# The reciprocal root of the first RMSNorm moves from the activations to the eviction of every projection bank

## The chip, the cores and the metric

The kernel runs on one core of a Trainium2 chip. The metric is the device time of one execution in microseconds (us); the runs are compared by their median. Engines are named as in the profile: PE is TensorE (matmuls; PEld its weight loads), DVE is VectorE, ACT is ScalarE, POOL is GpSimd, SP is the queue that issues most transfers.

## The reference

One layer of a hybrid decoder on 256 tokens of width 2048, all in fp32:

```python
n = rmsnorm(x, attn_norm[l])                 # x * rsqrt(mean(x*x) + eps) * attn_norm
u = n @ w_in[l]                              # 2048 -> 6928 columns
u_gdn, u_mlstm, u_rglru, u_rwkv = jnp.split(u, MIXER_SPLITS, axis=-1)
...                                          # four mixers, each a causal recurrence over the tokens
x = x + mix @ w_out[l]
n = rmsnorm(x, ffn_norm[l])
x = x + (jax.nn.silu(n @ ffn_w_gate[l]) * (n @ ffn_w_up[l])) @ ffn_w_down[l]
return rmsnorm(x, final_norm)
```

The reciprocal root is one number per token, so it can be multiplied in before the projection, on the activations, or after it, on each token's outputs. What the mixers do first with `u` matters here: gated delta rule (q, k, v) and mLSTM (q, k) put it through a causal convolution of four taps, RG-LRU puts one half through such a convolution with a bias and the other through a gelu, RWKV-7 mixes each token with the one before, and sixteen gate columns get a bias and go through softplus and the like.

## The kernel before, in words

**Products.** Every matrix product is made in three matmuls (`mm3`, lines 169 to 171) on operands split into a high and a low part: high x high, high x low, low x high. A weight block of 128 x 1024 is loaded by SP into one of four `raw` buffers, ACT copies its high part (`whi`) and DVE subtracts that to get the low part (`wlo`), lines 163 and 164. Both are issued through the helper `ch`, so the profile has them, and all else that `ch` issues, under lines 274 and 277. The activations lie transposed, 128 channels by 256 tokens in each of 16 tiles, as `nhi` and `nlo`.

**Input projection.** It goes in groups of 256 columns. A group takes four weight blocks and fills one PSUM bank of 512 columns (two halves of 128 channels by 256 tokens, or, with `tm=True`, two halves of 128 tokens by 256 channels). Three banks called `big` take turns. When a group is done its bank is emptied by a function decorated with `evict` (`shift_mix`, `conv`, `gelu2`, `silu2`), whose instructions are put 40 places forward in the priorities by which the order of work is laid out. That order is fixed when the program is built: a planner goes through the instructions by priority and by the times that it assumes, and gives each engine one list. Each engine then works through its list in order, and waits where an operand is not there.

**Start.** The sum of squares isn't known at first. So `setup` makes activations without the root (`un`: x times `attn_norm`, split into high and low, in four scratch pairs `UH`), and the first two groups (columns of the RWKV low-rank inputs and of r) run on them chunk by chunk as the transfers land. Meanwhile `squares` loads x once more in four pieces and sums the squares, `rstd` makes the root (`rs0`, one number per token on partitions), and `scales` spreads it by two matmuls over all partitions as the row `R` (128 x 256). The next two groups, k0 and v0, run on `un` too. The four banks are multiplied by `R` when `shift_mix` empties them (line 463). During v0, `normalise` (lines 282 to 290) makes the activations with the root: two multiplies on DVE (line 288), a copy to `nhi` on ACT (289) and a subtraction to `nlo` on DVE (290) for each pair of tiles. All later groups run on these, and their banks hold the finished `u`.

**Mixers.** Between weight blocks `group` calls `tick`, which steps generators: RWKV halves (`rw0`, `rw1`), RG-LRU, gates, delta rule and mLSTM halves, and two triangular solves on DVE (`solve_blocks`, lines 499 and 500). Their matmuls (line 409) take their places between the projection's in PE's list. After that come the output projection, the feed-forward part and the last norm; the change doesn't touch them.

**Lines of the evictions.** `shift_mix`: multiply 463 (first four banks), ACT copy 468, DVE 469. `conv`: ACT copy 759 or 761, three taps on DVE 763 for each half. `silu2`: 773, 774. `gelu2`: ACT 1165, 1166, then DVE 1167. Gates: 808. mLSTM v and output gate: 1430, 1433.

Of the kernel before, what the change touches and what calls it, by code (L numbers as in the profile page):

```python
# [7 lines left out]
F32 = mybir.dt.float32  # L8
F32R = mybir.dt.float32r
# [3 lines left out]
P = 128  # L13
T = 256
# [67 lines left out]
class Emitter:  # L82
# [115 lines left out]
    def setup(self):  # L198
        nc, A = self.nc, self.A
        self.pc = self.const([P, NCHAN], "chan")  # L200
        nc.scalar.dma_start(self.pc, A["chan"])
        c = 0
        for k, n in CHAN:
            self.PT[k] = self.pc[:, c : c + n]
            c += n
        ch = self.ch
        wu = self.const([P, 512], "wu", mybir.dt.bfloat16)
        ch("dve", nc.vector.memset, wu, 0.0)
        ch("act", nc.scalar.activation, self.const([P, 1], "wa"), wu[:, 0:1], AF.Square)
        z = self.mxl()  # L210
        for _ in range(WARM):
            ch("pe", nc.tensor.matmul, z, wu[:, 0:P], wu, start=True, stop=True)
        key = lambda g, c: ("w_in", 4 * c, 4, (RW + 1536, RW)[g], 256)
        raws, self.xt = {}, []

        def load(c):
            raws[0, c] = self.raw(*key(0, c))
            t = self.S(2)
            ch("sp", nc.sync.dma_start, t.rearrange("p (k t) -> p k t", k=4), A["xT"][:, 4 * c : 4 * c + 4, :])
            self.xt.append(t)  # L220
            raws[1, c] = self.raw(*key(1, c))

        load(0)
        load(1)
        self.nhi = self.xp.tile([P, KT, T], F32R, name="nhi", tag="nhi")
        self.nlo = self.xp.tile([P, KT, T], F32R, name="nlo", tag="nlo")
        self.UH = [(self.S(2), self.S(2)) for _ in range(4)]
        self.un = [tuple(t.bitcast(F32R)[:, (k % 4) * T : (k % 4) * T + T] for t in self.UH[k // 4]) for k in range(KT)]
        banks = [self.big(), self.big()]
        for c in range(4):  # L230
            ws = [self.halves(raws[0, c], *key(0, c))]
            for k in range(4 * c, 4 * c + 4):
                u, w = self.xt[c][:, (k % 4) * T : (k % 4) * T + T], self.PT["attn_norm"][:, k : k + 1]
                ch("act", nc.scalar.activation, self.un[k][0], u, AF.Copy, scale=w)
                ch("dve", nc.vector.scalar_tensor_tensor, self.un[k][1], u, w, self.un[k][0].bitcast(F32), op0=ALU.mult, op1=ALU.subtract)
            ws.append(self.halves(raws[1, c], *key(1, c)))
            for g, w in enumerate(ws):
                for l, r in ((0, 0), (0, 1), (1, 0)):
                    for m in range(2):
                        o = banks[g][:, m * T : m * T + T]  # L240
                        for kk in range(4):
                            k = 4 * c + kk
                            ch("pe", nc.tensor.matmul, o, w[l][:, kk, m * P : m * P + P], self.un[k][r], start=k == 0 and l == r == m == 0, stop=k == KT - 1 and l == 1, skip_group_check=True)
            if c < 2:
                load(c + 2)
        self.begun = self.chain
        self.chain = None
        self.ss = self.const([P, 2, 4], "ss")
        return banks

    def squares(self, c):

        nc = self.nc
        xs = self.S(2)
        nc.sync.dma_start(xs.rearrange("p (a n) -> p a n", a=2), self.A["x"].rearrange("(a p) d -> p a d", p=P)[:, :, c * 512 : c * 512 + 512])
        nc.scalar.activation(xs[:, 0:512], xs[:, 0:512], AF.Square, accum_out=self.ss[:, 0, c : c + 1])
        nc.vector.scalar_tensor_tensor(xs[:, 512:1024], xs[:, 512:1024], 1.0, xs[:, 512:1024], op0=ALU.mult, op1=ALU.mult, accum_out=self.ss[:, 1, c : c + 1])
        self.free(xs)
        if c == 3:
            self.rs0 = self.rstd(self.ss, "rs0")  # L260

    def scales(self, rs):

# [7 lines left out]
    def ch(self, key, fn, *a, **k):  # L271
# [6 lines left out]
        if self.chain is not None:  # L278
            self.chain[key] = i
        return i  # L280

    def normalise(self, u):

        nc = self.nc
        hi, lo = self.nhi[:, 2 * u : 2 * u + 2, :], self.nlo[:, 2 * u : 2 * u + 2, :]
        f = self.xt[u // 2].rearrange("p (k t) -> p k t", k=4)[:, 2 * (u % 2) : 2 * (u % 2) + 2, :]
        for j in range(2):
            nc.vector.scalar_tensor_tensor(f[:, j, :], f[:, j, :], self.PT["attn_norm"][:, 2 * u + j : 2 * u + j + 1], self.R[:, 0:T], op0=ALU.mult, op1=ALU.mult)
        nc.scalar.activation(hi, f, AF.Copy)
        nc.vector.tensor_tensor(lo, f, hi.bitcast(F32), op=ALU.subtract)  # L290

    def setup_consts(self):
        nc = self.nc
# [160 lines left out]
    return g  # L454


@evict
def shift_mix(em, bank, tiles, R=None):
    nc = em.nc
    X = em.S()  # L460
    if R is not None:
        b = em.S()
        nc.vector.tensor_tensor(b.rearrange("p (j t) -> p j t", j=2), bank.rearrange("p (j t) -> p j t", j=2), R[:, 0:T].unsqueeze(1).to_broadcast([P, 2, T]), op=ALU.mult)
        bank = b
    mu, mu1 = em.PT["rwkv_mu"], em.PT["mu1"]
    for j, ti in enumerate(tiles):
        u, o = bank[:, j * T : j * T + T], X[:, j * T : j * T + T]
        nc.scalar.activation(o, u, AF.Copy, scale=mu1[:, ti : ti + 1])
        nc.vector.scalar_tensor_tensor(o[:, 1:T], u[:, 0 : T - 1], mu[:, ti : ti + 1], o[:, 1:T], op0=ALU.mult, op1=ALU.add)
    if R is not None:  # L470
        em.free(b)
    return X


def rwkv_lora(em, bank):
    nc = em.nc
    X = shift_mix(em, bank, (12, 13), em.R)
    nc.scalar.activation(X[0:64, 0:T], X[0:64, 0:T], AF.Tanh)
    nc.scalar.activation(X[:, T : 2 * T], X[:, T : 2 * T], AF.Tanh, scale=0.5)
    nc.vector.tensor_scalar(X[:, T : 2 * T], X[:, T : 2 * T], 0.5, 0.5, op0=ALU.mult, op1=ALU.add)  # L480
    return X
# [270 lines left out]
def conv(em, bank, w, nt, tiles, bias=None):  # L752
    nc = em.nc
    X = em.S()
    for j, ti in enumerate(tiles):
        u, o = bank[:, j * T : j * T + T], X[:, j * T : j * T + T]
        tap = [w[:, i * nt + ti : i * nt + ti + 1] for i in range(4)]
# [3 lines left out]
            nc.scalar.activation(o, u, AF.Identity, scale=tap[3], bias=bias[:, ti : ti + 1])  # L761
        for d in range(1, 4):
            nc.vector.scalar_tensor_tensor(o[:, d:T], u[:, 0 : T - d], tap[3 - d], o[:, d:T], op0=ALU.mult, op1=ALU.add)
    return X


# [26 lines left out]
def gates_mm(em):  # L793
# [11 lines left out]
    gp = em.gp  # L805
    U, V = g[0:16, 0:T], g[0:16, T : 2 * T]
    N, B = g[0:16, 2 * T : 3 * T], g[0:16, 3 * T : 4 * T]
    nc.scalar.activation(U, o, AF.Identity, bias=gp[:, 0:1])
    nc.scalar.activation(gp[:, 1:2], gp[:, 1:2], AF.Exp)
    nc.scalar.activation(B, U, AF.Tanh, scale=0.5)  # L810
    nc.vector.tensor_scalar(B, B, 0.5, 0.5, op0=ALU.mult, op1=ALU.add)
# [349 lines left out]
def gelu2(em, bank):  # L1161

    nc = em.nc
    g, t = em.S(), em.S()
    nc.scalar.activation(g, bank, AF.Copy, scale=0.5)
    nc.scalar.activation(t, bank, AF.Square)
    nc.vector.tensor_scalar(t, t, 0.044715, 1.0, op0=ALU.mult, op1=ALU.add)
    nc.vector.tensor_tensor(t, t, g, op=ALU.mult)
    nc.scalar.activation(t, t, AF.Tanh, scale=2.0 * math.sqrt(2.0 / math.pi))
# [187 lines left out]
def hybrid(tc, A, out, dbg=None, parts=("rw", "gd", "ml", "rg", "tail", "ffn")):  # L1357
    nc = tc.nc
    with ExitStack() as ctx:
# [12 lines left out]
        def use(u):  # L1372
# [3 lines left out]
            elif u == 2:  # L1376
                with em.behind():
                    em.scales(em.rs0)
                early["L"] = rwkv_lora(em, lora)
            else:  # L1380
                early["R"] = shift_mix(em, r0, (0, 1), em.R)

        k0 = grp(RW + 512, acts=em.un, pre=use)
        LX, R0 = early["L"], early["R"]

        def norm(u):
            em.normalise(2 * u)
            em.normalise(2 * u + 1)

        v0 = grp(RW + 1024, acts=em.un, pre=norm)  # L1390
        K0 = shift_mix(em, k0, (4, 5), em.R)
        V0 = shift_mix(em, v0, (8, 9), em.R)
        em.free(em.R, *em.xt, *(t for u in em.UH for t in u))
        em.setup_solver()
        gates_load(em)
        if "rw" in parts:
# [18 lines left out]
        if "gd" in parts:  # L1415
            for hf in range(2):
                z = grp(GD + 1536 + 256 * hf, tm=True)
                SZ = em.S(c="L")
                silu2(em, SZ, z)
                Q, K, V = (conv(em, grp(GD + 512 * i + 256 * hf), em.PT["gdn_conv"], 12, (4 * i + 2 * hf, 4 * i + 2 * hf + 1)) for i in range(3))  # L1420
                em.spawn(f"gd{hf}", gdn_half(em, hf, Q, K, V, SZ))
                if hf == 0:
# [1 line left out]
        if "ml" in parts:  # L1424
            for hf in range(2):
# [1 line left out]
                V1 = v1s[:, 0:516].rearrange("p (a h n) -> p a h n", a=2, h=2)  # L1427
                nc.gpsimd.memset(V1[:, :, :, 128:129], 1.0)
                b = grp(ML + 1024 + 256 * hf, tm=True)
                nc.scalar.activation(V1[:, :, :, 0:128], b.rearrange("p (a h n) -> p a h n", a=2, h=2), AF.Copy)  # L1430
                b = grp(ML + 1536 + 256 * hf, tm=True)
                SO = em.S(c="L")
                nc.scalar.activation(SO, b, AF.Tanh, scale=0.5)
                nc.vector.tensor_scalar(SO, SO, 0.5, 0.5, op0=ALU.mult, op1=ALU.add)
                Q, K = (conv(em, grp(ML + 512 * i + 256 * hf), em.PT["mlstm_conv"], 8, (4 * i + 2 * hf, 4 * i + 2 * hf + 1)) for i in range(2))
                em.spawn(f"ml{hf}", mlstm_half(em, hf, Q, K, V1, SO, v1s))
        if dbg:
            while em.gens:
                em.tick()
# [24 lines left out]
```

## Time and profile before

| | |
|---|---|
| Median of 3 runs | 1270.41 us (1268.99 to 1271.3) |
| Profiled execution | 1272.06 us, its span 1270.3 us |
| PE busy | 1241.6 us, 98% of the span, 7216 matmuls |
| DVE busy | 781.4 us, 62% |
| ACT busy | 639.7 us, 50% |
| Mean granted PE clock | 0.990 |
| Chain that ended last | PE 88%, DVE 6%, ACT 2%, DMA 1%, issue 1% |

The span runs from the first to the last profiled instruction; the execution is a little longer. A row of a timeline gives the start and the duration in us, the engine, the line, the operation and the tiles (written <- read, buffer numbers left out), and in brackets how long the engine sat idle before it and what ended that. Matmuls and most DVE and ACT instructions overlap with the one before, so a run of them is read by its starts and not by the sum of the durations. A granted clock of 1.00 is PE's full speed, 0.50 half of it.

### The profile page before, as it was taken

What the parts mean: (1) busy time and instruction counts of PE and PEld (TensorE: products, weight loads), DVE (VectorE), ACT (ScalarE), POOL (GpSimd) and SP (SyncE); (2) the same over time, 40 slices, a digit from 0 to 9 for tenths busy, and PEclk for the clock granted to TensorE, in tenths of its full rate; (3) what the DMA queues carried; (4) which work ended last, traced back from release to release, by engine and by line L of the source; (5) the groups of instructions that cost most, each with busy time, mean ns of one, the idle gap of its engine ahead of it and who ended that gap; (6) DMA issues with size and microseconds to landing.
All of it is one profiled execution on the core that took longest, in us unless ns stands there. A gap on an engine that the chain in (4) does not pass through costs nothing.

```text
span 1270.3 us, 18343 instructions
## 1 busy us (share of the span) xinstructions
PE 1241.6 (98%) x7216; PEld 1074.4 (85%) x7216; DVE 781.4 (62%) x1087; ACT 639.7 (50%) x849; POOL 31.9 (3%) x65
## 2 busy tenths in 40 slices
PE   9999999999989999999999999999999999999997
PEld 8899999998988888888888888888888888878885
DVE  7876799666798775744454444445455455556554
ACT  7755784436644454644444444444444444445443
POOL 1100000000000100000000000000000000001000
PEclk9999999999999999999999999999999999999999
DMA  9554436344654356566666666666666666666663
GB/s 345 170 177 144 142 124 197 109 138 133 193 160 131 110 177 192 177 187 184 192 197 184 189 193 188 203 205 198 185 190 192 189 189 188 195 198 185 197 190 109
DMA packets 72198, 226.97 MB, mean 179 GB/s; under 512 B 15752, under 2 KB 16016, under 8 KB 72112
## 3 DMA queue, kind: packets, MB, share of 16 engines
q1 hardware_dynamic: 71504, 224.14, 57.2%
q0 software_dynamic: 464, 1.57, 0.5%
q8 instruction: 56, 0.92, 0.3%
q14 instruction: 30, 0.25, 0.1%
q10 hardware_dynamic: 144, 0.10, 0.0%
HBM read 222.49 MB, written 3.28 MB: 178 GB/s over the span
## 4 chain that ended last, share of the span: by engine, by line
PE 88%; DVE 6%; ACT 2%; DMA 1%; issue 1%; POOL 0%; DVEq 0%; POOLq 0%; SPq 0%; ACTq 0%
PE big L171 14%; PE big L170 14%; PE big L169 13%; PE mx L169 10%; PE mx L171 10%; PE mx L170 10%; PE mx L409 4%; PE mxl L171 3%; PE mxl L169 3%; PE mxl L170 3%; DVE wlo L274 2%; PE big L277 2%; DVE sD L499 1%; DVE sD L500 1%; PE mx L413 1%
## 5 line engine op out<-in xcount | busy, mean ns | idle before, releaser
L274 DVE TENSOR_TENSOR wlo<-raw,whi 128x1024 fp32r<-128x1024 f32 x396 | 485.6, 1227 | 376.8 <-ACT whi L274 375.8
L274 ACT ACTIVATE whi<-raw 128x1024 fp32r<-128x1024 f32 x396 | 418.2, 1057 | 447.4 <-PE big L171 271.7
L170 PE MATMUL big<-wlo,nhi 128*128 128x512 f32 (+1 forms) x464 | 162.2, 350 | 0.9 <-DVE wlo L274 0.9
L169 PE MATMUL big<-whi,nhi 128*128 128x512 f32 (+1 forms) x464 | 161.9, 349 | 0.1
L171 PE MATMUL big<-whi,nlo 128*128 128x512 f32 (+1 forms) x464 | 161.7, 349 | 0.0
L171 PE MATMUL big<-nhi,wlo 128*128 128x256 f32 x544 | 158.8, 292 | 3.0 <-DVE wlo L274 3.0
L170 PE MATMUL big<-nlo,whi 128*128 128x256 f32 x544 | 158.6, 292 | 0.0
L169 PE MATMUL big<-nhi,whi 128*128 128x256 f32 x544 | 157.8, 290 | 0.0
L169 PE MATMUL mx<-whi,nhi 128*128 128x512 f32 x352 | 138.0, 392 | 0.0
L171 PE MATMUL mx<-whi,nlo 128*128 128x512 f32 x352 | 137.0, 389 | 0.0
L170 PE MATMUL mx<-wlo,nhi 128*128 128x512 f32 x352 | 137.0, 389 | 0.0
L171 PEld LDWEIGHTS big<-nhi,wlo 128*128 128x128 f32 x544 | 106.0, 195 | 4.9 <-DVE wlo L274 3.2
L170 PEld LDWEIGHTS big<-nlo,whi 128*128 128x128 f32 x544 | 105.8, 194 | 1.9 <-issue 0.7
L169 PEld LDWEIGHTS big<-nhi,whi 128*128 128x128 f32 x544 | 105.9, 195 | 1.4 <-issue 0.3
L170 PEld LDWEIGHTS big<-wlo,nhi 128*128 128x128 f32 x464 | 89.0, 192 | 12.3 <-DVE wlo L274 1.5
L169 PEld LDWEIGHTS big<-whi,nhi 128*128 128x128 f32 x464 | 89.0, 192 | 11.1 <-ACT whi L274 0.3
L171 PEld LDWEIGHTS big<-whi,nlo 128*128 128x128 f32 x464 | 89.1, 192 | 10.9
L169 PE MATMUL mx<-whi,sA 128*128 128x512 f32 x212 | 82.9, 391 | 0.7 <-ACT sA L1178 0.7
L170 PE MATMUL mx<-wlo,sA 128*128 128x512 f32 x212 | 82.5, 389 | 0.0
L171 PE MATMUL mx<-whi,sA 128*128 128x512 f32 x208 | 80.9, 389 | 0.0
L171 PEld LDWEIGHTS mx<-whi,nlo 128*128 128x128 f32 x352 | 66.1, 188 | 13.8
L170 PEld LDWEIGHTS mx<-wlo,nhi 128*128 128x128 f32 x352 | 66.1, 188 | 13.3
(424 smaller groups left out, 1786.4 us busy)
## 6 DMA issues: line engine op xcount, KB each, us to landing
raw<-in_units SPq DMA_DIRECT2D x404, 512.0 KB, 3.6
sD<-in_x SPq DMA_DIRECT2D x8, 512.0 KB, 5.1
sD<-in_xT SPq DMA_DIRECT2D x4, 512.0 KB, 6.3
out_y<-sD SPq DMA_DIRECT2D x8, 256.0 KB, 3.0
sA<-in_final_norm POOLq DMA_DIRECT2D x4, 256.0 KB, 5.9
sD<-in_lora SPq DMA_DIRECT2D x1, 512.0 KB, 6.6
sD<-in_rglru POOLq DMA_DIRECT2D x1, 512.0 KB, 3.8
dr<-sD SPq DMA_DIRECT2D x2, 256.0 KB, 4.2
```

Source lines behind the costliest of these rows:

```text
L169: i = nc.tensor.matmul(out, ahi, bhi, start=start, stop=False, skip_group_check=True)
L170: nc.tensor.matmul(out, ahi, blo, start=False, stop=False, skip_group_check=True)
L171: self.last_mm = nc.tensor.matmul(out, alo, bhi, start=False, stop=stop, skip_group_check=True)
L274: i = fn(*a, **k)
L277: i = fn(*a, **k)
L409: return self.em.nc.tensor.matmul(*a, **k)
L413: return self.em.nc.tensor.transpose(*a, **k)
L499: nc.vector.tensor_tensor(tv, col, row, op=ALU.mult)
L500: nc.vector.tensor_tensor(inv[:, j + 1 : n, 0:b], inv[:, j + 1 : n, 0:b], tv, op=ALU.add)
```

## The change

The input projection runs on `nhi` and `nlo` without the root, from the first group to the last: `setup` writes `un` straight into `nhi` and `nlo`, `normalise` goes, and each eviction multiplies by the root. Where channels are on partitions that is a DVE multiply of the whole bank with the broadcast row `R` (new function `scaled`, before `conv` and every `shift_mix`; folded into one instruction in `gelu2`). Where tokens are on partitions (`tm=True`) it is the scale operand of ACT, one instruction per half, since each half has its own tokens; `rs0h` is half the root, for the tanh of the mLSTM output gate. `R` is kept until the input projection is over; the transposed x is freed at the end of `setup`.

```diff
@@ setup
-        self.UH = [(self.S(2), self.S(2)) for _ in range(4)]
-        self.un = [tuple(t.bitcast(F32R)[:, (k % 4) * T : (k % 4) * T + T] for t in self.UH[k // 4]) for k in range(KT)]
+        self.un = [(self.nhi[:, k, :], self.nlo[:, k, :]) for k in range(KT)]
...
+        self.free(*self.xt)
@@ squares
             self.rs0 = self.rstd(self.ss, "rs0")
+            self.rs0h = self.const([P, 2], "rs0h")
+            nc.vector.tensor_scalar(self.rs0h, self.rs0, 0.5, None, op0=ALU.mult)
@@ normalise: removed
-        for j in range(2):
-            nc.vector.scalar_tensor_tensor(f[:, j, :], f[:, j, :], self.PT["attn_norm"][:, 2 * u + j : 2 * u + j + 1], self.R[:, 0:T], op0=ALU.mult, op1=ALU.mult)
-        nc.scalar.activation(hi, f, AF.Copy)
-        nc.vector.tensor_tensor(lo, f, hi.bitcast(F32), op=ALU.subtract)
@@
+def scaled(em, bank):
+
+    b = em.S()
+    em.nc.vector.tensor_tensor(b.rearrange("p (j t) -> p j t", j=2), bank.rearrange("p (j t) -> p j t", j=2), em.R[:, 0:T].unsqueeze(1).to_broadcast([P, 2, T]), op=ALU.mult)
+    return b
@@ shift_mix (now for every bank) and conv
+    bank = b = scaled(em, bank)
...
+    em.free(b)
@@ gates_mm
-    nc.scalar.activation(U, o, AF.Identity, bias=gp[:, 0:1])
+    nc.vector.tensor_tensor(U, o, em.R[0:16, 0:T], op=ALU.mult)
+    nc.scalar.activation(U, U, AF.Identity, bias=gp[:, 0:1])
@@ gelu2
-    nc.scalar.activation(g, bank, AF.Copy, scale=0.5)
-    nc.scalar.activation(t, bank, AF.Square)
+    nc.vector.scalar_tensor_tensor(g.rearrange("p (j t) -> p j t", j=2), bank.rearrange("p (j t) -> p j t", j=2), 0.5, em.R[:, 0:T].unsqueeze(1).to_broadcast([P, 2, T]), op0=ALU.mult, op1=ALU.mult)
+    nc.scalar.activation(t, g, AF.Square, scale=2.0)
@@ hybrid
-        k0 = grp(RW + 512, acts=em.un, pre=use)
+        k0 = grp(RW + 512, pre=use)
...
-        v0 = grp(RW + 1024, acts=em.un, pre=norm)
+        v0 = grp(RW + 1024)
...
-                silu2(em, SZ, z)
+                with em.tc.high_priority(offset=EPRIO):
+                    for a in range(2):
+                        nc.scalar.activation(SZ[:, a * T : a * T + T], z[:, a * T : a * T + T], AF.Copy, scale=em.rs0[:, a : a + 1])
+                silu2(em, SZ)
...
-                nc.scalar.activation(V1[:, :, :, 0:128], b.rearrange("p (a h n) -> p a h n", a=2, h=2), AF.Copy)
+                for a in range(2):
+                    nc.scalar.activation(V1[:, a, :, 0:128], b[:, a * T : a * T + T].rearrange("p (h n) -> p h n", h=2), AF.Copy, scale=em.rs0[:, a : a + 1])
...
-                nc.scalar.activation(SO, b, AF.Tanh, scale=0.5)
+                for a in range(2):
+                    nc.scalar.activation(SO[:, a * T : a * T + T], b[:, a * T : a * T + T], AF.Tanh, scale=em.rs0h[:, a : a + 1])
```

## Rows read from the trace of the kernel before

**Rows 1.** Busy time (instructions) by stretch, then PE's clock, DMA share, GB/s:
```profile
44.00:62.00 18.00, 14.98 (x107) 13.63 (x106) 17.23 (x33) 15.74 (x28) 2.67 (x3) 0.96 0.46 147
...
165.00:200.00 35.00, 33.15 (x259) 31.06 (x258) 33.91 (x76) 25.00 (x35) 0.95 (x1) 0.96 0.45 145
200.00:300.00 100.00, 100.00 (x1030) 92.46 (x1030) 70.87 (x138) 46.39 (x66) 0.74 (x3) 1.00 0.50 153
...
350.00:403.00 53.00, 47.30 (x375) 46.62 (x374) 49.49 (x106) 22.77 (x38) 2.57 (x4) 0.97 0.49 144
```

**Rows 2.** What PE waited for: us in total, times, longest us:
```profile
PE big L171 <- DVE wlo L274: 3.0, 1, 3.0
...
PE mx L409 <- DVE sA L774: 2.8, 1, 2.8
PE mx L409 <- DVE sB L422: 2.3, 1, 2.3
PE mx L413 <- DVE sA L846: 1.9, 1, 1.9
...
PE mx L409 <- ACT sB L421: 0.8, 1, 0.8
```

**Rows 3.** Timeline of PE around its longest wait, 57 to 68 us:
```profile
57.89 0.28 PE L170 MATMUL big<-sD,whi 128*128 128x256 f32 x1
58.01 0.28 PE L171 MATMUL big<-sD,wlo 128*128 128x256 f32 x1
61.30 0.58 PE L171 MATMUL big<-nhi,wlo 128*128 128x256 f32 x1 [3.02 <-DVE wlo L274]
...
67.44 0.29 PE L169 MATMUL big<-nhi,whi 128*128 128x256 f32 x1
```

**Rows 4.** Busy time by stretch, behind two waits, as in rows 1:
```profile
62.00:67.00 5.00, 5.00 (x25) 5.00 (x25) 5.00 (x8) 1.06 (x2) 0.00 (x0) 0.50 0.74 241
...
373.00:377.00 4.00, 1.15 (x9) 1.10 (x9) 3.85 (x6) 1.57 (x2) 0.52 (x1) 1.00 0.47 141
```

**Rows 5.** Groups by line and shape: busy us, mean ns | idle before, releaser:
```profile
L759 ACT ACTIVATE sA<-big,chan 128x256 f32<-128x256 f32 x20 | 9.3, 465 | 14.5 <-DVE sA L763 9.3 <-PE big L171 4.7 <-PE mx L409 0.5
...
L288 DVE SCALAR_TENSOR_TENSOR sD<-sD,chan,sA 128x256 f32<-128x256 f32 x16 | 6.8, 482 | 0.0
L1283 DVE SCALAR_TENSOR_TENSOR sA<-big,rs,sA 128x512 f32<-128x512 f32 x8 | 5.9, 742 | 0.0
L290 DVE TENSOR_TENSOR nlo<-sD,nhi 128x512 fp32r<-128x512 f32 x8 | 5.3, 690 | 0.0
L469 DVE SCALAR_TENSOR_TENSOR sA<-sA,chan,sA 128x255 f32<-128x255 f32 x8 | 3.4, 482 | 0.7 <-ACT sA L468 0.7
L469 DVE SCALAR_TENSOR_TENSOR sA<-big,chan,sA 128x255 f32<-128x255 f32 x6 | 2.9, 479 | 1.1 <-ACT sA L468 1.1
L463 DVE TENSOR_TENSOR sA<-big,sA 128x512 f32<-128x512 f32 x4 | 2.7, 686 | 0.0
...
L817 DVE TENSOR_TENSOR sD<-sD 16x256 f32<-16x256 f32 x1 | 0.4, 404 | 0.0
```

**Rows 6.** Pieces of the chain that ended last: start us, us, what:
```profile
39.03 1.20 DVE sA L463 x2
...
49.94 4.38 DMA raw<-in_units
...
312.90 0.40 DVE sA L763
```

**Rows 7.** Timeline, the first RWKV half: DVE's split and PE's matmul on it:
```profile
67.77 0.67 DVE L422 TENSOR_TENSOR sB<-sA,sB 128x512 fp32r<-128x512 f32 x1
...
80.41 0.39 PE L409 MATMUL mx<-sB,exact 128*128 128x512 f32 x1
```

**Rows 8.** Timeline of ACT, line 468 with a multiplied and an unmultiplied bank:
```profile
39.66 1.71 ACT L468 ACTIVATE sA<-sA,hw 128x256 f32<-128x256 f32 x4 [3.89 <-DVE sA L463]
...
78.20 0.47 ACT L468 ACTIVATE sA<-big,hw 128x256 f32<-128x256 f32 x1 [1.32 <-DVE sA L469]
```

More of the change, by code (lines that the diff above doesn't have):

```diff
@@ L280, in ch @@
         return i
[L282 to L286, printed above, removed]
-        for j in range(2):
-            nc.vector.scalar_tensor_tensor(f[:, j, :], f[:, j, :], self.PT["attn_norm"][:, 2 * u + j : 2 * u + j + 1], self.R[:, 0:T], op0=ALU.mult, op1=ALU.mult)
-        nc.scalar.activation(hi, f, AF.Copy)
-        nc.vector.tensor_tensor(lo, f, hi.bitcast(F32), op=ALU.subtract)
     def setup_consts(self):
@@ L454, in evict, with shift_mix @@
     return g
+def scaled(em, bank):
+    b = em.S()
+    em.nc.vector.tensor_tensor(b.rearrange("p (j t) -> p j t", j=2), bank.rearrange("p (j t) -> p j t", j=2), em.R[:, 0:T].unsqueeze(1).to_broadcast([P, 2, T]), op=ALU.mult)
+    return b
 @evict
-def shift_mix(em, bank, tiles, R=None):
+def shift_mix(em, bank, tiles):
     nc = em.nc
     X = em.S()
[L461 to L464, printed above, removed]
+    bank = b = scaled(em, bank)
     mu, mu1 = em.PT["rwkv_mu"], em.PT["mu1"]
@@ L469, in shift_mix @@
         nc.vector.scalar_tensor_tensor(o[:, 1:T], u[:, 0 : T - 1], mu[:, ti : ti + 1], o[:, 1:T], op0=ALU.mult, op1=ALU.add)
-    if R is not None:
-        em.free(b)
+    em.free(b)
     return X
@@ L476, in rwkv_lora @@
     nc = em.nc
-    X = shift_mix(em, bank, (12, 13), em.R)
+    X = shift_mix(em, bank, (12, 13))
     nc.scalar.activation(X[0:64, 0:T], X[0:64, 0:T], AF.Tanh)
@@ L754, in conv @@
     X = em.S()
+    bank = b = scaled(em, bank)
     for j, ti in enumerate(tiles):
@@ L763, in conv @@
             nc.vector.scalar_tensor_tensor(o[:, d:T], u[:, 0 : T - d], tap[3 - d], o[:, d:T], op0=ALU.mult, op1=ALU.add)
+    em.free(b)
     return X
@@ L1380, in use @@
             else:
-                early["R"] = shift_mix(em, r0, (0, 1), em.R)
-        k0 = grp(RW + 512, acts=em.un, pre=use)
+                early["R"] = shift_mix(em, r0, (0, 1))
+        k0 = grp(RW + 512, pre=use)
         LX, R0 = early["L"], early["R"]
-        def norm(u):
-            em.normalise(2 * u)
-            em.normalise(2 * u + 1)
-        v0 = grp(RW + 1024, acts=em.un, pre=norm)
-        K0 = shift_mix(em, k0, (4, 5), em.R)
-        V0 = shift_mix(em, v0, (8, 9), em.R)
-        em.free(em.R, *em.xt, *(t for u in em.UH for t in u))
+        v0 = grp(RW + 1024)
+        K0 = shift_mix(em, k0, (4, 5))
+        V0 = shift_mix(em, v0, (8, 9))
         em.setup_solver()
@@ L1436, in hybrid @@
                 em.spawn(f"ml{hf}", mlstm_half(em, hf, Q, K, V1, SO, v1s))
+        em.free(em.R)
         if dbg:
```

## The prediction

> **What bounds the kernel now.** I read the page first, then the busy time by stretch, then TensorE's waits, then the timeline around each of them. TensorE (PE) is busy 1241.6 of 1270.3 us, and in the long stretch 200 to 300 us it is never idle [rows 1]. The change takes no matmul away, so it can only win or lose where PE stands still or runs slowly. There are few such places. PE's longest wait is for the low half of one weight block, made by VectorE (DVE) on line 164 (in the rows L274, the helper that records it): 3.0 us [rows 2]. [...] The pitch is back to 0.12 from 67.44. Between 61.30 and 67.44 lie 28 steps. At the old pitch matmul 29 would have started at 58.13 + 28 x 0.12 = 61.49; it started at 67.44. So this place costs 5.95 us.
>
> Its cause is DVE. In 44 to 62 us DVE is busy 17.2 of 18 us [rows 1]: it normalises all sixteen activation tiles a second time there (lines 288 and 290), between two low halves of weights. The other waits over 1.8 us belong to the mixers and are for DVE too [rows 2]: 1.9 at about 195 (line 846, gate scan), 2.3 at 316 (line 422), 2.8 at 373 (line 774). In 165 to 200 us DVE is busy 33.9 of 35, in 350 to 403 us 49.5 of 53 [rows 1]. In those two stretches DVE is as full as it is in the first.
>
> **The change, part by part.**
>
> Removed: sixteen multiplies of line 288 (6.8 us busy) and eight subtractions of line 290 (5.3 us), 12.1 us of DVE in all [rows 5], and eight ScalarE (ACT) copies of line 289. What is left for DVE in 44 to 62 us is 17.2 - 12.1 = 5.1 us, low halves of weights and two evictions, and PE wants one low half each 2.9 us (24 matmuls at 0.12). The stall has nothing left to make it: **-5.95 us**. What could be late next is the weight block's transfer: one of them takes 4.38 us in the chain [rows 6]. I cost that at nothing, since four blocks are in flight and 4.38 / 4 = 1.1 us a block; it is a rival below.
>
> Is the gain handed back at the next wait? After 62 us the first mixer starts. Its line 422 is done by 68.4, and PE comes to the matmul that needs it at 80.41 [rows 7], 12 us later. PE arriving 6 us earlier still finds it ready, and what follows in that mixer starts from PE's matmul and moves with it. So the gain holds.
>
> Added on DVE: one multiply per bank for R1, K1 and V1 and for twelve convolution banks, 15 of the kind of line 463 (0.69 us each, 128x512, bank times a broadcast row); two multiply-multiplies in gelu2 in place of ACT copies, like line 1283 (0.74 each); one 16x256 multiply in the gates, like line 817 (0.40) [rows 5]. That is 10.3 + 1.5 + 0.4 = 12.2 us, as much as goes away, only later. Two in a row take 1.20 us in the chain [rows 6], so one on a full DVE costs 0.6. Most of them lie under matmuls: in 200 to 300 us PE never waits [rows 1], and 0. Where PE waits for DVE today:
> - the wait of 0.8 at 92 us, for a copy that ACT makes behind a run of DVE work [rows 2]: the multiply for K1 falls there, **+0.6**.
> - 165 to 200 us: the gelu multiply and the gates' multiply, 0.74 + 0.40 = **+1.1**.
> - 350 to 403 us: two convolution banks (mLSTM's q and k, first half), 2 x 0.6 = **+1.2**.
> - 417 to 421 us, ahead of the waits in the tail of the delta rule: one bank, **+0.6**.
>
> Bounds of each are 0 (PE's wait has another cause) and the wait doubled.
>
> Moved: the taps no longer read the PSUM bank. Today the two halves of a bank take turns: with R1 the second ACT copy sits idle 1.32 us until DVE's tap is done, while with lora and r0, which are multiplied first, four ACT copies run in one piece of 1.71 us [rows 8]. After the change all evictions look like the latter. In 312 to 320 us, a stretch in which DVE holds PE, two taps of 0.40 [rows 6] stand on the chain only because their half came late; they go: **-0.8**. The bounds are 0 and the whole wait there, 2.3 [rows 2].
>
> [...]
>
> At nothing: the first pass writes into nhi and nlo instead of four scratch pairs, with the same instructions. The loads of x for the squares find free slots earlier, but what they feed waits for a place in PE's order. The 128x2 half of the root falls where DVE is idle for that. The SP queue issues the same transfers in the same order. The split scalings on ACT (gated delta z, mLSTM v and o) add some 0.5 us each for ten pieces, less the six whole ones that they replace or lengthen; ACT is busy 25.0 of 35 and 22.8 of 53 us in the full stretches [rows 1], and not what PE waits for. If that cover is gone, at most 0.9 us (two pieces of 0.47 as in [rows 8]) stands in one chain.
>
> **Sum:** -5.95 + 0.6 + 1.1 + 1.2 + 0.6 - 0.8 = -3.25 us. The profiled execution took 1272.06 (span 1270.3 and 1.8 around it), so it would take 1268.8; the median of the runs is 1270.41, 1.65 below the profiled one, and comes to **1267.2**.
>
> **Rivals.**
>
> A, *the gain in full and more*: short convolutions. If the half-bank turns are what delays the silu of line 774, the wait of 2.8 at 373 goes as well, and the additions cost nothing: -5.95 - 0.8 - 2.8 = -9.5, 1261. For it speaks that ACT's copies in the convolutions (line 759) sit idle 9.3 us for the other half's taps [rows 5]; against it, DVE is full there, so that what comes earlier makes another DVE step later. [...]
>
> B, *no change*: the weight transfers end last in 44 to 70 us. The chain has one of 4.38 us there [rows 6]. If PE then waits 2 us or so and its clock falls again, about half of the 5.95 comes back: -3.25 + 3.0 = -0.2, 1270.2. Against it: that transfer was issued late because DVE freed its buffer late.
>
> C, *slower*: DVE's full stretches hold PE so long that its clock falls where it doesn't today. Three waits lie near that: 0.8 at 92, 2.8 at 373 (clock 1.00 after it [rows 4]), and the tail of the delta rule. After the 3.0 us the clock stayed at half speed for about 6 us, that is 5.95 - 3.17 = 2.8 us lost beyond the idle time itself. Three such falls are 8.4, and -3.25 + 8.4 = +5.2: 1275.6. It decides when a wait that is short today passes some 3 us, that is if the convolutions' multiplies, emitted with a head start over the mixers' work, push the solver's steps and the silus back by 2 us or more instead of the 0.6 to 1.2 that they take themselves. For it: DVE at 94 to 97% in two stretches, and an order that is laid out anew for the whole program. Against: the removed work is as long as the added.
>
> **How the numbers follow.** What can be told from no change is about 0.2%, 2.5 us. Chances: the forecast 0.42 (from -1 to -5, two thirds of it beyond -2.5), A 0.17, B 0.18, C 0.23. Faster: 0.28 + 0.17 = 0.45. Same: 0.14 from the forecast, 0.15 from B: 0.29. Slower: C and 0.03 of B, 0.26. The range goes from A, 1261, to a little over C's price, 1276; the forecast's own range is 1265 to 1270.
>
> **What would show it.** Right: no wait of PE between 57 and 70 us and clock 1.00 there; lines 288 to 290 gone; PE's rw0 matmul about 6 us earlier; ACT copies of a convolution back to back; the wait at 195 longer by about 1 us. Rival A: no wait on line 774. B: PE or ACT waiting for raw in 50 to 70 us. C: more stretches at clock 0.50 than the kernel before has after 90 us, or longer waits for DVE in 165 to 200 and 350 to 403 us. I am wrong in the main step if PE still idles near 58 us.

## The result and the profile after

Nine runs of the changed kernel took 1278.8 us in the median (1272.99 to 1280.51), nine of the kernel before on the same chip 1271.3: a ratio of 1.0054 [1.0037, 1.007], 6.9 us slower. The profiled execution took 1279.74 us, its span is 1278.0, 7.7 longer than before.

The page, first line of its busy times:

```profile
PE 1246.7 (98%) x7216; PEld 1077.1 (84%) x7216; DVE 781.3 (61%) x1082; ACT 636.3 (50%) x846; POOL 31.6 (2%) x65
```

DVE's work is the same as before (781.3 against 781.4 us). The multiply of line 463 [rows 5] is line 452 now, 18 times where it was 4 (one more falls under another tile name), and all 24 taps of the first kind read SBUF, busy us, mean ns as in [rows 5]:

```profile
L452 DVE TENSOR_TENSOR sA<-big,sA 128x512 f32<-128x512 f32 x18 | 12.3, 686 | 3.1 <-PE big L171 3.1
L759 DVE SCALAR_TENSOR_TENSOR sA<-sA,chan,sA 128x255 f32<-128x255 f32 x24 | 10.8, 478 | 1.9 <-ACT sA L757 1.0 <-ACT sA L755 0.8
```

PE issues the same 7216 matmuls, is busy 5.1 us longer (1246.7 - 1241.6) and idle 2.6 us longer (31.3 against 28.7). The 5.1 fit the clock: the mean granted clock fell from 0.990 to 0.986, which is about 25 us at 0.50 before and 36 after. In the changed kernel 128x256 matmuls start 0.12 us apart at 257.1 to 257.4 us, at 1.00, and 0.21 apart at 262 to 263.7 us, at 0.50; in the kernel before it is 0.21 from 61.7 to 67.4 us, at 0.50, and 0.12 behind that. By these pitches 0.09 / 0.21 of the 11 us is lost, 4.7 us, an estimate.

Busy time by stretch, columns as in [rows 1]: four stretches of [rows 1], then two that matter now:

```profile
44.00:62.00 18.00, 18.00 (x150) 17.87 (x149) 12.50 (x14) 9.97 (x14) 0.00 (x0) 1.00 0.75 248
165.00:200.00 35.00, 33.74 (x278) 31.91 (x277) 34.44 (x77) 24.94 (x39) 0.95 (x1) 1.00 0.47 145
200.00:300.00 100.00, 98.80 (x971) 89.24 (x970) 69.06 (x136) 43.27 (x61) 0.75 (x3) 0.95 0.45 140
350.00:403.00 53.00, 48.14 (x384) 47.48 (x383) 49.65 (x104) 24.23 (x42) 2.58 (x4) 0.97 0.49 146
258.00:268.00 10.00, 10.00 (x52) 8.60 (x53) 4.20 (x9) 0.13 (x1) 0.00 (x0) 0.53 0.31 101
429.00:436.00 7.00, 5.74 (x25) 5.45 (x26) 2.27 (x9) 2.17 (x10) 0.69 (x1) 0.51 0.07 27
```

The first row is the gain: PE is busy all of 18 us at a clock of 1.00, and DVE has 12.5 us of work where it had 17.2. In 165 to 200 and 350 to 403 us PE is no worse off than before (busy 33.74 and 48.14 us against 33.15 and 47.30). The loss shows from 200 to 300 us, where PE never waited [rows 1]: it does now, and its clock is 0.53 for 10 us. Near 430 us the clock is 0.51. What PE waited for, columns as in [rows 2] (lines are those of the changed kernel: 401 was 409, 771 was 774, 413 was 421):

```profile
PE mx L401 <- DVE sB L983: 4.0, 1, 4.0
PE mx L401 <- ACT sB L413: 3.7, 2, 3.0
PE mx L401 <- DVE sA L1063: 3.4, 2, 2.5
PE mx L405 <- DVE sB L994: 2.3, 1, 2.3
...
PE mx L401 <- DVE sA L771: 1.4, 1, 1.4
...
PE mx L405 <- DVE sA L844: 1.3, 1, 1.3
PE big L171 <- DVE wlo L276: 1.0, 1, 1.0
```

The 3.0 us for `wlo` of [rows 2] are gone, and 1.4 of the 2.8 on the silu. In their place stand the wait of 4.0 us for line 983, at the end of the delta rule, and one of 3.0 for ACT (413). The waits for 994 and for 1063 (mLSTM) were there before, as 996 and 1065; the one for 1065 is missing from the prediction's list of the waits over 1.8 us:

```profile
PE mx L409 <- DVE sA L1065: 2.9, 2, 2.5
...
PE mx L409 <- DVE sB L996: 1.5, 1, 1.5
```

PE's timeline at three of these places and at the first mixer:

```profile
75.01 0.39 PE L401 MATMUL mx<-sB,exact 128*128 128x512 f32 x1
...
255.54 0.28 PE L170 MATMUL big<-nlo,whi 128*128 128x256 f32 x1
256.86 0.39 PE L171 MATMUL big<-nhi,wlo 128*128 128x256 f32 x1 [1.04 <-DVE wlo L276]
...
429.81 2.08 PE L401 MATMUL mx<-sB,sB 128*128 128x128 f32 x8 [4.03 <-DVE sB L983]
...
443.30 0.69 PE L405 MATMUL mx<-ident,sB 128*128 128x128 f32 x2 [2.25 <-DVE sB L994]
443.65 0.78 PE L169 MATMUL big<-whi,sA 128*128 128x512 f32 x1
```

The first row answers to [rows 7]: 75.01 against 80.41, so PE is 5.4 us ahead after the start. The last is the first matmul of the output projection; it started at 436.48 before. From there both kernels need the same (834.4 and 833.8 us). All that was lost was lost between 75 and 444 us, and DVE's timeline shows two places of it:

```profile
349.62 0.69 DVE L452 TENSOR_TENSOR sA<-big,sA 128x512 f32<-128x512 f32 x1 [0.69 <-PE big L171]
350.59 1.23 DVE L276 TENSOR_TENSOR wlo<-raw,whi 128x1024 fp32r<-128x1024 f32 x1 [0.28 <-DMA sB<-Md]
351.73 2.45 DVE L759 SCALAR_TENSOR_TENSOR sA<-sA,chan,sA 128x255 f32<-128x255 f32 x6
354.21 0.18 DVE L494 TENSOR_TENSOR sD<-sD,sD 32x31 f32<-32x31 f32 x1
...
407.36 1.12 DVE L498 COPY sD<-sD 32x1024 f32<-32x1024 f32 x1
...
426.60 2.45 DVE L759 SCALAR_TENSOR_TENSOR sA<-sA,chan,sA 128x255 f32<-128x255 f32 x6
429.08 0.42 DVE L971 COPY sL<-mx 64x256 f32<-64x256 f32 x1
429.42 0.59 DVE L983 TENSOR_SCALAR sB<-mx,GT 128x128 f32<-128x128 f32 x2
```

Line 452 is the multiply. The taps of a convolution (759), six in one run because both halves are there at once, stand ahead of the first step of the triangular solve (494), and again, at 426.60, ahead of the step for which PE waits 4.03 us. Line 498 is the last instruction of the solve of the delta rule. The same two points before:

```profile
350.31 0.18 DVE L499 TENSOR_TENSOR sD<-sD,sD 32x31 f32<-32x31 f32 x1 [0.34 <-DMA sD<-dr]
...
403.13 1.13 DVE L503 COPY sD<-sD 32x1024 f32<-32x1024 f32 x1
```

The solve starts 3.9 us later than before, although PE was ahead, and ends 4.2 us later; what comes after it takes 3.5 us more. 4.2 + 3.5 = 7.7.

Not all of this is the order at the solve's start. SP issues the load of the solve's input 1.5 us later than before, although PE had been 5.4 us ahead, so most of the lead was gone by then. After, then before:

```profile
346.65 0.34 SPq L930 DMA_DIRECT2D sD<-dr  x1
```

```profile
345.19 0.34 SPq L932 DMA_DIRECT2D sD<-dr  x1
```

And up to 350 us PE idles as long as before, 6.2 us; what differs is its clock. Again after, then before, columns as in [rows 1]:

```profile
70.00:350.00 280.00, 273.82 (x2337) 255.54 (x2336) 212.14 (x387) 166.32 (x236) 3.70 (x7) 0.97 0.47 145
```

```profile
70.00:350.00 280.00, 273.76 (x2374) 256.51 (x2373) 209.56 (x380) 168.60 (x236) 4.22 (x8) 0.99 0.48 148
```

In what follows, the end of the solve (the start of its last instruction) is one mark by which kernels are compared. It does not stand for the time: several runs below end the solve early and are slow.

### The profile page after: what moved, and what is told of

It reads as the page before. It is cut to its first block, busy times and chain, and to the rows that moved or that the text cites. A ratio compares the mean times of both kernels' runs of the same rounds, so it can differ in the third digit from the quotient of the medians.

```text
span 1278.0 us, 18349 instructions
## 1 busy us (share of the span) xinstructions
PE 1246.7 (98%) x7216; PEld 1077.1 (84%) x7216; DVE 781.3 (61%) x1082; ACT 636.3 (50%) x846; POOL 31.6 (2%) x65
## 4 chain that ended last, share of the span: by engine, by line
PE 87%; DVE 7%; ACT 3%; issue 2%; DMA 1%; POOL 0%; SPq 0%; DVEq 0%; POOLq 0%; ACTq 0%
PE big L171 13%; PE big L170 13%; PE big L169 13%; PE mx L169 10%; PE mx L171 10%; PE mx L170 10%; PE mx L401 4%; PE mxl L171 3%; PE mxl L170 3%; PE mxl L169 3%; DVE wlo L276 2%; PE big L279 2%; DVE sD L494 1%; DVE sD L495 1%; DVE sA L759 1%
## 5 line engine op out<-in xcount | busy, mean ns | idle before, releaser
L171 PE MATMUL big<-nhi,wlo 128*128 128x256 f32 x608 | 176.6, 291 | 1.0 <-DVE wlo L276 1.0
L170 PE MATMUL big<-nlo,whi 128*128 128x256 f32 x608 | 176.5, 290 | 0.0
L169 PE MATMUL big<-nhi,whi 128*128 128x256 f32 x608 | 175.9, 289 | 0.2 <-ACT whi L276 0.2
L171 PEld LDWEIGHTS big<-nhi,wlo 128*128 128x128 f32 x608 | 117.6, 194 | 3.5 <-DVE wlo L276 1.2
L170 PEld LDWEIGHTS big<-nlo,whi 128*128 128x128 f32 x608 | 117.5, 193 | 2.8 <-issue 1.3
L169 PEld LDWEIGHTS big<-nhi,whi 128*128 128x128 f32 x608 | 117.4, 193 | 2.6 <-issue 0.7
```

The lines of the kernel that those rows point to most:

```text
L169: i = nc.tensor.matmul(out, ahi, bhi, start=start, stop=False, skip_group_check=True)
L170: nc.tensor.matmul(out, ahi, blo, start=False, stop=False, skip_group_check=True)
L171: self.last_mm = nc.tensor.matmul(out, alo, bhi, start=False, stop=stop, skip_group_check=True)
```

## The experiments

Three theories at first. M: the multiplies cost DVE time in front of the mixers, about one for one. H: the gain of the start is handed back by the mixers whatever is added. O: any new order of the lists is worth several us. The expectations of e1 to e4 name them differently: "taps" (what costs is that a convolution's six taps run in one piece), "ahead" (PE's lead is lost by itself, close to H) and "order" (O). T, in e9, is that copies and taps behind the multiply are what costs. Ratios below are to the kernel before, on the same chip.

**e1, half-bank turns back.** ACT's copy of the second half was put behind the first half's last tap:

```diff
+            if j:
+                turn.enter_context(em.tc.issue_after(last.ins))
```

> The kernel after, with the two halves of each convolution made to take turns again: the second half's ACT copy is held behind the first half's last tap, as the shared bank did it before. Multiply and all work stay. Theory taps (the six taps of a convolution now come in one run of 2.4 us, laid ahead of the recurrences' short DVE steps, and PE waits for those where it has no other work: at 426 and 441 us and before the solver): most of the 7.5 us goes, 1268 to 1273. Theory order (the whole list of work is laid out anew by any edit, and the waits fall by chance): anywhere from 1266 to 1285, with waits in other places. Theory ahead (PE's lead from the start is lost by itself, since a chain through the solver on DVE and not PE's own pace sets when the output projection starts): no change, 1276 to 1281.

1275.48, 1.0042 [1.0026, 1.0057]. The six taps still ran in one piece of 2.45 us ahead of the solve, at 350.27, and PE's waits were the same (4.0, 2.3). The edit did not take apart what it was to take apart, so it tells nothing on the bunching.

**e2, taps without the head start.** Only the multiply keeps the 40 places:

```diff
-@evict
 def conv(em, bank, w, nt, tiles, bias=None):
...
+    with em.tc.high_priority(offset=EPRIO):
+        bank = b = scaled(em, bank)
```

> The kernel after, where only the multiply that empties a convolution's bank is put forward; ACT copies and taps have the mixers' own priority. Theory taps: the taps fall behind the recurrences' steps, the solver starts by 351 instead of 354 us and the waits at 426 and 441 shrink: 1266 to 1273. Theory order: anywhere from 1266 to 1285. Theory ahead: 1276 to 1281.

1273.89, 1.003 [1.0018, 1.0042]. The solve started at 344.13 and ended at 400.46 + 1.14, some 7 us earlier than in the changed kernel, with the same instructions. Where the taps stand matters, but the kernel is still slower than before.

**e3, no multiply in the convolutions; e4, the multiply alone.** e3 is the changed kernel without it (the root is left out there). e4 is the kernel before with each of the twelve banks multiplied by ones:

```diff
-    bank = b = scaled(em, bank)
```

> The kernel after without the multiply in the twelve convolutions, whose taps read the bank as before (the root is left out of these channels); the first eight banks, gelu2, the gates and the scaled copies stay as in the kernel after. Twelve multiplies of 0.69 us less on DVE. Theory taps, and the plain sum of the prediction: the gain of the start (5.95 us) is kept, 1264 to 1268. Theory ahead: the start is won and lost again by the solver's chain, 1269 to 1274. Theory order: anywhere from 1264 to 1285.

> The kernel before, normalisation kept, with one multiply by ones in front of each of the twelve convolutions, whose taps then read SBUF. This is the added part alone (twelve multiplies and the taps off the bank). Theory taps: slower than before by about what the change lost behind its start, 7.5 + 5.95 = 13 us, 1280 to 1286, with the solver starting late and waits in the delta rule's tail. The plain sum: +2 to +3 us, 1273 to 1275. Theory ahead: since PE has no lead here, 1271 to 1275. Theory order: anywhere from 1266 to 1285.

e3: 1267.72, 0.9976 [0.9964, 0.9988]. e4: 1274.84, 1.0026 [1.0013, 1.0038]. So all the rest of the change gains 3.1 us, and the twelve multiplies cost 3 to 4 us by themselves and some 10 within the change (1.0054 - 0.9976 = 0.0078). e4 came out where its expectation has the plain sum of the prediction, and its solve ends no later than before (402.61 against 403.13).

**e5, e6: only some of the twelve.** Left out ahead of the mLSTM's four (e5), or of the delta rule's six (e6); the root is left out there.

> The changed kernel with the multiply left out ahead of the four convolutions of the mLSTM (their taps read the bank again; the root is left out there), kept ahead of the other eight. If the cost sits in the banks that come in 350 to 445 us (theory M: the multiplies count where DVE is full), the second loss goes and the first stays: TensorE at half clock near 257 us as in the changed kernel, no wait of 4 us near 425, 1271 to 1273. If the gain of the start is handed back by the mixers whatever is added late (theory H), 1276 to 1278. If it is the new order of the lists as such (theory O), anything from 1270 to 1279, with the waits at other places than in the changed kernel.

> The changed kernel with the multiply left out ahead of the six convolutions of the gated delta rule, kept ahead of the RG-LRU's two and the mLSTM's four. Theory M: the first loss goes (no half clock near 257 us) and the solver of the delta rule starts some 2 us earlier, the waits near 425 stay: 1272 to 1275. Theory H: 1276 to 1278. Theory O: anything from 1270 to 1279.

e5: 1274.85, 1.0041 [1.0023, 1.0058]; e6: 1276.2, 1.0046 [1.0027, 1.0066]. Each gives back only a part of the 10 us: it is not one group of banks. In e5 the wait at 429 was gone, as M expected, but its profiled execution ran at a granted clock of 0.50 right there, in 411 to 437 us. In e6 the solve ends at 396.45 us, 6.7 earlier than before, and its profiled execution, the fastest of its ten, still took 1270.21: there the wait for a late step of the delta rule (line 983, in e6 985) is 4.1 us. This wait is 3.1 to 4.1 us in every run whose mLSTM taps read a multiplied bank with the head start, and at most 2.9 in the others.

**e8, the stall put back.** The normalisation's DVE instructions at their old places, on a tile that nobody reads:

> The changed kernel with the stall at the start put back: the sixteen multiplies and eight subtractions are issued on DVE again at the places of the normalisation, on a tile that nobody reads after them. It adds 12.1 us of DVE work and, at 58 us, 3.2 us of idle time and 6 us of half clock on TensorE. If the gain at the start counts in full in the changed kernel (theory M), 1278.8 + 6 = 1284 to 1286. If it was handed back by the mixers (theory H), 1277 to 1280, with the losses near 257 and 425 us gone or smaller.

1280.51, 1.0079 [1.0056, 1.0102], 1.7 us above the changed kernel by the medians, 3.2 by the ratios. PE waited 2.3 us for `wlo` at 58 us, not the 3.0 of before. Between the two theories' numbers and with too wide an interval to tell: inconclusive.

**e9, e15: the multiplies as work that nobody waits for.** In e9 the twelve multiplies stay, but ACT and the taps read the bank; in e15 there are two per bank. The root is left out in both.

```diff
-    bank = b = scaled(em, bank)
+    b = scaled(em, bank)
```

> The changed kernel, its twelve multiplies ahead of convolutions kept as DVE work, but nobody reads what they write: ACT's copies and the taps read the bank as in the kernel before, so the root is left out there. DVE does the same work as in the changed kernel (12 x 0.69 = 8.3 us more than without the multiplies, which took 1267.7). If it is the work on a full DVE that costs (theory M), 1276 to 1279. If it is that a convolution's copies and taps now have to stand behind the multiply and run in one piece (theory T), 1268 to 1271. If the lists' order as such decides (theory O), anything between, with the waits at new places.

> The kernel whose twelve multiplies nobody reads (1275.8), with two of them in place of one ahead of each convolution: 8.3 us more DVE work in the same places. One for one (theory M): 1284, with longer waits of TensorE near 370 and 425 us. If the cost came from their being there at all (their place in the lists, a clock that falls or doesn't): 1274 to 1279.

e9: 1275.76, 1.0038 [1.0025, 1.0051]. e15: 1284.35, 1.0103 [1.0078, 1.0128]. With none (e3), twelve and twenty-four multiplies the solve ends here, one row of DVE's timeline for each kernel:

```profile
399.54 1.12 DVE L498 COPY sD<-sD 32x1024 f32<-32x1024 f32 x1
```

```profile
406.80 1.14 DVE L498 COPY sD<-sD 32x1024 f32<-32x1024 f32 x1
```

```profile
414.38 1.12 DVE L498 COPY sD<-sD 32x1024 f32<-32x1024 f32 x1
```

Twelve multiplies of 0.69 us are 8.3 us; ten of them, 6.9 us, lie ahead of the solve's end (the last two start at 424.04 and 435.71 us in e9). The first twelve move that end by 7.3, the next twelve by 7.6; the ratios rise by 0.0062 and 0.0065, 7.9 and 8.3 us. In this kernel the added DVE work goes into the time one for one. On PE it shows as idle time and as clock: in 165 to 300 and 350 to 403 us PE idles 5.3, 6.7 and 10.6 us in the three kernels, and the mean granted clock of their profiled executions is 0.994, 0.987 and 0.985. What e15's PE waited for:

```profile
PE mx L401 <- DVE sA L772: 3.8, 2, 3.1
PE big L171 <- DVE wlo L276: 3.3, 2, 2.5
```

The weights' low halves are among it: with enough work ahead of them on DVE even the projection waits.

**e14, the convolutions' multiplies alone in the changed kernel.** The root is left out everywhere else, and those banks are emptied as before.

> The changed kernel with only the twelve convolutions' multiplies left of what it adds: the root is left out in R1, K1 and V1, in gelu2, in the gates and in the three banks that ACT scales, which are emptied as in the kernel before. It saves 2.1 + 1.5 + 0.4 = 4.0 us of DVE work and ten pieces of ACT's. If the multiplies cost 11 us because they add up with this other work: 1270 to 1273. If it is H, or the convolutions alone: 1276 to 1279.

1278.61, 1.0063 [1.0041, 1.0084]: no different from the whole change. The split scalings on ACT, gelu2, the gates and R1, K1, V1 cost nothing that shows; the two intervals leave room for some 3 us.

**e7, e13, e17: the stall removed in another way, then the multiplies.** e7 keeps normalised activations and spreads the normalisation over two groups:

```diff
-        v0 = grp(RW + 1024, acts=em.un, pre=norm)
+        v0 = grp(RW + 1024, acts=em.un, pre=em.normalise)
...
-            R1 = shift_mix(em, grp(RW + 256), (2, 3))
+            r1 = grp(RW + 256, acts=em.un, pre=lambda u: em.normalise(4 + u))
+            R1 = shift_mix(em, r1, (2, 3), em.R)
```

> Not the change, but the kernel before with the normalisation spread over two groups (v0 and the RWKV r of the second half, which then runs on the activations without the root too and gets one more multiply) in place of one. DVE's load in 44 to 62 us falls from 17.2 to about 11 us, so the stall at 58 us goes; added is one multiply of 0.69 us, not fifteen. Theory M: 1270.4 - 5.95 + 0.6 = 1265. Theory H: the mixers hand back half of it or more: 1267.5 to 1271. Theory O: anything within 4 us of 1266.

1266.14, 0.9969 [0.9955, 0.9983]: faster than both kernels. The reason is not the one expected. DVE's load in 44 to 62 us did not fall:

```profile
44.00:62.00 18.00, 18.00 (x144) 17.07 (x144) 17.63 (x30) 12.85 (x21) 0.95 (x1) 1.00 0.55 175
```

DVE is busy 17.63 of 18 us, and PE does not wait, because the low halves now come up in its list soon enough: six of them start in that stretch, four before. e13 adds the twelve multiplies by ones to e7, e17 the same with the row R in place of the ones (so the root stands in twice there).

> The kernel with the normalisation spread over two groups (1266.1, no stall at the start), and ahead of each of its twelve convolutions a multiply of the bank by ones, with the taps reading the product. If the multiplies cost the same with and without the stall: 1266.1 + 4.0 = 1270. If the gain of the start is handed back once they are there (theory H): 1274 to 1277.

> The kernel with normalised activations and no stall, its convolutions' banks multiplied by the row of the root (so the root stands in twice there) in place of ones, the row kept until the end of the projection. If the operand matters: 1274 to 1278 against 1270.4 with ones. If not: 1268 to 1272.

e13: 1270.4, 1.0012 [0.9988, 1.0035], which speaks against H: by the medians the multiplies cost 4.3 us on a kernel without the stall as they cost 4.0 on one with it (e4); by the ratios 5.5 and 3.3. e17: 1278.57, 1.0064 [1.0039, 1.009]. The same twelve banks multiplied in instructions of the same length (689 ns in e13, 685 in e17), and the medians are 8 us apart (6.6 by the ratios). DVE's timeline, e13 first, then e17:

```profile
333.71 0.28 DVE L919 TENSOR_TENSOR sB<-mx,sB 128x128 f32<-128x128 f32 x1
...
341.12 1.22 DVE L274 TENSOR_TENSOR wlo<-raw,whi 128x1024 fp32r<-128x1024 f32 x1 [1.66 <-ACT whi L274]
342.94 0.18 DVE L499 TENSOR_TENSOR sD<-sD,sD 32x31 f32<-32x31 f32 x1 [0.59 <-DMA sD<-dr]
```

```profile
335.76 0.28 DVE L919 TENSOR_TENSOR sB<-mx,sB 128x128 f32<-128x128 f32 x1
...
344.47 0.69 DVE L756 TENSOR_TENSOR sA<-big,sA 128x512 f32<-128x512 f32 x1 [0.69 <-PE big L171]
345.44 1.23 DVE L274 TENSOR_TENSOR wlo<-raw,whi 128x1024 fp32r<-128x1024 f32 x1 [0.28 <-DMA sB<-Md]
346.59 2.45 DVE L766 SCALAR_TENSOR_TENSOR sA<-sA,chan,sA 128x255 f32<-128x255 f32 x6
349.07 0.18 DVE L499 TENSOR_TENSOR sD<-sD,sD 32x31 f32<-32x31 f32 x1
...
402.24 1.12 DVE L503 COPY sD<-sD 32x1024 f32<-32x1024 f32 x1
```

Line 919 writes the solve's input; SP stores it and loads it back. In e13 the solve's first step comes next in DVE's list and waits only for that load. In e17 the input is ready 2.0 us later, and the list has the bank's multiply, which waits for PE, a weight's low half and six taps ahead of the first step: 6.1 us later in all. SP, again e13 and then e17:

```profile
339.22 0.34 SPq L936 DMA_DIRECT2D sD<-dr  x1
```

```profile
341.56 0.34 SPq L936 DMA_DIRECT2D sD<-dr  x1
```

The load back is issued 2.3 us later; with e13's 3.7 us from issue to first step the solve could have begun at 345.3. The other 3.8 us are DVE's list. Its instructions start in that order, the first step 0.03 us behind the last tap. The changed kernel has e17's order (351.73 and 354.21 above). The solve ends 3.6 us apart in the two (398.68 in e13), the spans 4.8; the rest of the 8 us is between profiled executions and medians. This order is not the whole cause: e17's solve ends 0.9 us earlier than that of the kernel before (402.24 against 403.13), and e17 is slower.

**e16, ones in the changed kernel.** If R as an operand made the difference, this should have been fast.

> The changed kernel with its convolutions' banks multiplied by ones in place of the root (left out there). Same number of multiplies, same tiles written. If the operand matters (a row that is kept, its shape in the planner's order): 1270 to 1274, and the solve of the delta rule ends near 399 to 403 us as with ones elsewhere. If not: 1276 to 1280, the solve's end at 405 to 408.

1279.58, 1.007 [1.0046, 1.0094]: it isn't the operand. Ones are in the good order in e13 and in the bad one here. The solve ends at 403.86 us, earlier than expected and 0.7 later than before, and the time is no better for it.

**e10, e11: another order, the same work.** The mixers' matmuls 21 places back instead of 20, in the changed kernel and in the one before.

> The changed kernel with the constant that puts the mixers' matmuls back in the priorities at 21 places in place of 20; no instruction is added or taken away, some matmuls and DVE instructions change places in their lists. Theory O (an order laid out anew is worth several us either way): off from 1278.8 by 3 us or more. Theory M or H: within 2 us, 1277 to 1281, with the waits near 255 and 425 us still there.

> The kernel before with the same constant at 21 in place of 20, nothing else. Theory O: off from its 1270.4 by 3 us or more. Theory M or H: within 2 us, with the stall at 58 us unchanged.

1277.52, 1.0051 [1.0034, 1.0068], and 1271.9, 1.0021 [0.9998, 1.0044]. Not any new order is worth several us: in both, PE's longest waits are on the same lines as without the edit (983, 994 and 1063; 774, 422 and 846). O as stated falls. But e10 happens to have e13's order at the solve's start:

```profile
348.94 0.18 DVE L494 TENSOR_TENSOR sD<-sD,sD 32x31 f32<-32x31 f32 x1
...
349.59 0.69 DVE L452 TENSOR_TENSOR sA<-big,sA 128x512 f32<-128x512 f32 x1 [0.23 <-PE big L171]
```

The first step stands ahead of the multiply and starts 5.3 us earlier than in the changed kernel, the solve ends 2.3 us earlier (405.03), and the time is the same within the noise. e4 and e15 have that order too. So the order at this place does not by itself account for the difference between e13 and e17.

**e18, the changed kernel with the solve's steps put forward; e12, e7 with its taps put back.**

> The changed kernel with the steps of the triangular solves put 40 places forward in the priorities, as the evictions are; no instruction added or left out. If the time follows the solve's end (it starts behind six taps in one run at 351.7 to 354.2 us): the solve ends 2 to 6 us earlier and the time is 1272 to 1276. If the loss is elsewhere (the clock, the tail alone): 1277 to 1280.

> The kernel with the normalisation spread over two groups (1266.1), and in it the taps of the convolutions without the head start of 40 places; ACT's copies keep it. With the taps behind the mixers' steps DVE serves what TensorE waits for first: where that was done to the changed kernel it gave 5 us. Theory M: 1262 to 1265, the waits at 367 and 383 us shorter. If the banks, which are freed later, hold the projection up in place of that: 1267 to 1270. Theory O: anything within 4 us of 1266.

e18: 1282.65, 1.0083 [1.005, 1.0116], with the six taps still ahead of the first step; neither range of the expectation held. The solve ended at 402.21, 5.2 us earlier than in the changed kernel, and the time got no better: its profiled execution, 1285.53 us, had a mean granted clock of 0.979 where the changed kernel's had 0.986. Two more of its six runs took 1285.45 and 1286.54 us at the same mean clock, 0.979; the other three 1275.55 to 1279.85 us at 0.986 to 0.990. e12: 1267.41, 0.9978 [0.996, 0.9997], no better than e7. So an earlier solve alone does not decide the time; the clock counts too.

## Why the prediction was wrong

- **The start: right.** No wait of PE in 44 to 62 us, clock 1.00, and the first mixer's matmul 5.4 us earlier where 5.95 was forecast. DVE was left with 12.5 us of work there, not 5.1: PE no longer waits and takes nine low halves where it took four.
- **"So the gain holds": wrong for this kernel.** It holds up to the solve when no multiply is added (e3, e7: the solve ends 3.6 and 6.4 us earlier than before). With the change's twelve multiplies it ends 4.2 us later.
- **The step that failed: the additions, priced at 0.6 + 1.1 + 1.2 + 0.6 us because "Most of them lie under matmuls".** The sum looked where PE waits in the kernel before and put the multiplies in 200 to 300 us, where PE never waits, at 0. Inside the change the twelve multiplies of the convolutions, 1.8 us of that sum, cost 8 us, one for one (e3, e9, e15); 12 x 0.69 = 8.3 was in [rows 5]. In the stretch priced at 0 PE now waits 1.2 us and has 10 us at 0.53. The bound taken from the nearest row, the wait doubled, could not reach that, because the cost is not tied to the old waits. That a multiply and its taps push back the mixers' steps behind them in DVE's list is shown at two places, at the solve's start and at 426.60. That all of the 8 us goes this way is not shown: up to 350 us PE's idle time is that of before and the clock is what differs, and the wait of 1.04 us ahead of the 10 us at 0.53 has no multiply near it (217.40 and 268.09 are the nearest).
- **The wait of line 846 was forecast to grow by 1.1 us: wrong.** It fell from 1.9 to 1.3 (line 844 now).
- **The vanished turns, -0.8: wrong.** The taps do run without turns, but the wait near 316 us is 3.0, and no longer for DVE: ACT (line 413) is what PE waits for there. The prediction had ruled ACT out as what PE waits for. The split scalings are not the reason, since e14 has none of them and the same wait. And taps without turns are a run of six, 2.45 us in one piece, ahead of the solve's first step.
- **Removed equals added: right, and no argument.** DVE's sum is the same to 0.1 us. What was removed had made one wait; what was added stands ahead of many steps for which PE waits.
- **At nothing (ACT's split scalings, PSUM or SBUF): no cost shows.** e14 prices the rest of the change at nothing, within some 3 us. The sum has no term for the taps that leave PSUM, and the runs show none: line 469 takes 479 ns from the bank and 482 from SBUF before [rows 5], a convolution's tap 478 from SBUF in the changed kernel and 478 from the bank in e9.
- **Rival C came nearest.** Its place (steps of the solve and the mixers pushed back), its second half (clock) and its size, 1275.6, were near. Its condition, a wait that passes some 3 us, was met at 430 us (4.03) and not at 257, where the clock was 0.53 behind a wait of 1.04. The 3 us were the author's estimate; in the kernel before the clock was 0.50 in 197.2 to 200.5 us too, behind the wait of 1.9. B did not show: PE has no wait in 50 to 70 us, and ACT only one for `raw`, 2.2 us that end at 50.12.

What stays open: why the twelve multiplies cost 3 to 6 us in e4 and e13, by medians or ratios, and 8 to 12 in the rest. Around the solve the order differs between e13 and e17, but e10 has the good order and no better time. How the 8 us divide between DVE's order and PE's clock, and what makes either fall one way or the other, was not found.

## What to carry to other kernels

Price work added to an engine by what stands behind it in that engine's own list, and not only by the waits of the engine it feeds: here twelve multiplies beside a PE that was busy 98% cost their whole length inside the change, and about half of it elsewhere (e4, e13). Before work is moved off a stall, ask whether the stall needs less work or only another order: spreading the same normalisation over two groups (e7) removed it, with DVE as full as before, for one more multiply. When an order is laid out anew, look up what stands ahead of the first step of each serial chain, and test whether the time follows it: here it did in e2 and not in e10 or e18.

## What was not expected of the hardware

PE's granted clock stayed at 0.50 for 26 us behind a wait of 2.16 us at 407 in e5, and for 23 us behind one of 1.69 at 405 in e12:

```profile
411.00:437.00 26.00, 25.36 (x179) 22.54 (x179) 12.02 (x29) 5.88 (x16) 0.69 (x1) 0.50 0.36 106
```

```profile
408.50:431.50 23.00, 23.00 (x171) 20.64 (x170) 10.59 (x23) 3.91 (x7) 0.00 (x0) 0.50 0.28 95
```

In e12 PE is busy all of 23 us at 0.50; that profiled execution is the slowest of its ten, 1277.72 us against 1265.76 to 1267.98. A 2.8 us wait before was followed by 1.00 [rows 4], a 1.04 us wait after by 0.53. Runs of one kernel differ by it: e5's ten go from 1271.26 us at a mean granted clock of 0.991 to 1280.14 at 0.982, and e13's from 1267.55 at 0.994 to 1278.73 at 0.981. In these runs the length of a wait alone does not tell whether the clock falls, nor for how long.
